# Moving GpSimd's arithmetic to VectorE, and building the low parts of the attention weights by accumulating DMA

## The chip, the core and the metric

The kernel runs on one core of a Trainium2 chip. The core has a matrix engine (TensorE, "PE" in the profile), VectorE ("DVE"), ScalarE ("ACT"), GpSimd ("POOL"), and SyncE ("SP"), which here only issues DMAs. Each engine works through its own queue in order and waits at semaphores for the others. The metric is the device time of one execution in microseconds; lower is better.

## What is computed

The reference is one inference step of a two-layer decoder, in float32, over 512 prompt tokens and 8 x 8 sample tokens:

```python
rq, rk, rv, rg, sq, sk, sv, mq, g_r, g_s, g_m = in_proj(xp, w_in[l], pos_p)
ret_o, s_p = retention_prompt(rq, rk, rv)            # per head pair
swa_o = swa_prompt(sq, sk, sv, attn_sinks[l])        # window 128
mk, mv = mem_kv(mem_prompt, w_mem_kv[l])
mem_o = mem_attend(mq, mk, mv)
ret_b = (silu(rg) * group_norm(ret_o, gn_g)) @ w_br_ret
swa_b, mem_b = swa_o @ w_br_swa, mem_o @ w_br_mem
merged = sigmoid(g_r) * ret_b + sigmoid(g_s) * swa_b + sigmoid(g_m) * mem_b
x = layer_norm(ALPHA * x + merged @ w_out, ln1_g, ln1_b)
h = square(relu(x @ w_up))
x = layer_norm(ALPHA * x + h @ w_down, ln2_g, ln2_b)
```

The model width is 1024. The sample tokens go through the same weights with caches of their own. The weights of a layer are some 80 MB, and nearly all the work is the product of the 576 tokens with them.

## The kernel before

**Units.** The weights of a layer are cut into 154 units of 128 x 1024 float32 (512 KB). `unit_order` gives their sequence: mk, mv (memory keys and values, four each); for each of four head pairs rk, rq, rv, rv, rg, rg; sv, sk, sq; gr and br; mq; gs, bs, gm, bm; wo (eight); then for four chunks of the MLP eight up and eight dn. "Unit u" counts through both layers. Tokens are handled as two groups, A and B, of 288 columns each.

**Precision.** PE multiplies in the format fp32r, which keeps fewer bits than float32. So each operand is split into a rounded high part and a low part, the rest. `gemm` does three matmuls for each of a unit's eight slots: high by high, low by high, high by low. The unit's low part is therefore needed from its second matmul on.

**The life of a unit.** `fetch` (L516) lets SP load the raw unit. `split` (L522) makes high and low. For up and dn units the high part is a copy on ACT, the low part is first -raw by an ACT activation with scale -1, and then a DMA issued by POOL adds the raw unit to it: an accumulating DMA. (The scaled copy is rounded as the high part is, so raw added to it leaves the rest.) For all other units `split_into` is used with `flexible=True`: `rounded` casts on ACT or DVE, and `pick` has the subtraction done on DVE or POOL.

**What sets the order.** The program is written by a builder that keeps a clock of its own: `Clock` gives every operation a cost and an end on its engine, `Filler` writes side work (attention, norms) between the matmuls when its inputs are due by that clock. `rounded` and `pick` choose the engine that would be done sooner by that clock. `tick` writes the next split when ACT is free by the clock, but a unit may be at most `cap` ahead of the last one whose matmuls are finished (3 in the attention part, up to 5 in the MLP). If PE's code comes to a unit that is not yet split, `run` writes the split there. Units are fetched two ahead of the split. Once written, the order is fixed, and the chip follows it in every queue.

**Side work that the change touches.** `norm_ev` (L701) is the LayerNorm spread over the last projection: accumulations, squares, the shift and the affine step. `retention` (L877) has four masked copies `vz` on POOL for each head pair. The rest are splits of activations in the memory attention, the MLP and elsewhere.

**Tiles.** All large tiles have the tag T, in a ring of 38 buffers. pg and pa are PSUM banks, u and t are small tiles, and accA, accB, rc, s and ln belong to the norm. Since every operation is written through the helper `Timed`, all rows carry its line, L337, and the tiles and shapes have to tell them apart.

Of the kernel before, what the change touches and what calls it, by code (L numbers as in the profile page):

```python
# [8 lines left out]
F32 = mybir.dt.float32  # L9
# [15 lines left out]
EPS = 1e-5  # L25
# [396 lines left out]
class Builder:  # L422
# [75 lines left out]

    def pick(self, *ins, bias=0.0):
        n = ins[0].free_size()  # L500
        return self.soonest((("vector", 0.068 + n / 960.0 + bias), ("gpsimd", 0.15 + n / 480.0)), *ins)

    def rounded(self, hi, src):
# [4 lines left out]
    def split_into(self, hi, lo, src, flexible=False):  # L508
        if flexible:
            self.rounded(hi, src)  # L510
        else:
            self.nc.scalar.copy(hi, src)
        e = self.pick(hi) if flexible else self.nc.vector
        e.tensor_tensor(lo, src, hi.bitcast(F32), ALU.subtract)

# [6 lines left out]
    def split(self, u):  # L522
        raw = self.raw.pop(u)
        k = unit_order()[u % UNITS]
        hi = self.tile([P, 8, P], F32R)
        lo = self.tile([P, 8, P], F32R)
        if k[0] in ("up", "dn"):
            self.nc.scalar.copy(hi, raw)
            self.nc.scalar.activation(lo, raw, AF.Copy, scale=-1.0)
            self.nc.gpsimd.dma_start(lo, raw, accum_op=ALU.add)  # L530
        else:
            self.split_into(hi, lo, raw, True)
        self.w[u] = (hi, lo)
# [166 lines left out]

    def norm_ev(self, g, y, l, gi, eps, out, scale=None, bias=1.0):  # L701

# [23 lines left out]
        def shift():  # L726
            pm = self.bank("a")[:, :n]
            yield from mean(pm, st["acc"])
            yield (pm,)
            st["c"] = self.u(n)  # L730
            V.tensor_scalar(st["c"], pm, 4.0, None, ALU.mult)
            cb = st["c"].unsqueeze(1).to_broadcast([P, 4, n])
            self.pick(y[1], st["c"], bias=bias).tensor_tensor(y[1], y[1], cb, ALU.subtract)

        def half():
            c = st.pop("c")
            V.tensor_tensor(y[0], y[0], c.unsqueeze(1).to_broadcast([P, 4, n]), ALU.subtract)
# [4 lines left out]
            self.pick(sq[:, 0:2], sq[:, 2:4], bias=bias).tensor_tensor(sq[:, 0:2], sq[:, 0:2], sq[:, 2:4], ALU.add)  # L742
            self.pick(sq[:, 0], sq[:, 1], bias=bias).tensor_tensor(sq[:, 0], sq[:, 0], sq[:, 1], ALU.add)
            self.pick(st["s2"], sq[:, 0], bias=bias).tensor_tensor(st["s2"], st["s2"], sq[:, 0], ALU.add)

        def last():
# [28 lines left out]
            def mult(i):  # L775
                j, k = pieces[i]
                if i == 2 and out is not None:
                    V.tensor_tensor(y[1], y[1], mb, ALU.subtract)
                e = G if i == 3 and out is None else V
                e.tensor_tensor(y[j][:, k], y[j][:, k], rb, ALU.mult)  # L780
                return y[j][:, k]
# [8 lines left out]
            def end(i):  # L790
                j, k = pieces[i]
                for q in (k.start, k.start + 1):
                    affine(4 * j + q, y[j][:, q], y[j][:, q], V)
                h = out[g]["h"][j][:, k]
                self.pick(y[j][:, k], h).tensor_tensor(out[g]["l"][j][:, k], y[j][:, k], h.bitcast(F32), ALU.subtract)
            if out is not None:
# [28 lines left out]
        def ev(m, ps):  # L825
# [7 lines left out]
            if m == 0:  # L833
# [4 lines left out]
                return  # L838
            self.pick(yt, st["acc"], bias=0.0 if m in (1, 7) else bias).tensor_tensor(st["acc"], st["acc"], yt, ALU.add)
            if m == 1:  # L840
                st["shift"] = shift()
                self.fill.add(st["shift"], 1)
            if m == 4:
                st["s2"] = self.tile([P, 512], tag={"A": "s", "B": "rc"}[g], bufs=1)[:, :n]
                S.activation(st["s2"], yt, AF.Square)
                st["half"] = half()
                self.fill.add(st["half"], 1)
            elif m > 4:
                sq = self.u(n)
                S.activation(sq, yt, AF.Square)  # L850
                if m == 7:
                    self.fill.finish(st["half"])
                if m == 7:
                    self.fill.flush()
                    self.pick(sq, st["s2"]).tensor_tensor(st["s2"], st["s2"], sq, ALU.add)
                    st["last"] = last()
                    self.fill.add(st["last"], 0)
                else:
                    self.fill.later(lambda: self.pick(sq, st["s2"], bias=bias).tensor_tensor(st["s2"], st["s2"], sq, ALU.add),
                                    2.0, sq)  # L860
# [16 lines left out]
    def retention(self, l, p, qk, rv, rvs, sg, GR):  # L877
# [159 lines left out]
        for g_ in "AB":  # L1037
            src = wt[:, :, OFF[g_]:OFF[g_] + NG[g_]]
            hi, lo = GR[g_]["h"][h0 // 4][:, m:m + 2, :], GR[g_]["l"][h0 // 4][:, m:m + 2, :]
            S.copy(hi, src)  # L1040
            yield (hi,)
            self.pick(src, hi, bias=1.0).tensor_tensor(lo, src, hi.bitcast(F32), ALU.subtract)

# [29 lines left out]
    def hi_lo(self, hi, lo, src):  # L1073

        self.nc.scalar.copy(hi, src)
        yield (hi,)
        e = self.nc.vector if src.space == PSUM else self.pick(src, hi)
        e.tensor_tensor(lo, src, hi.bitcast(F32), ALU.subtract)

# [134 lines left out]
    def mem_prompt(self, h, mq, mk, mv, ME):  # L1214
# [7 lines left out]
        for i, g in enumerate("AB"):  # L1222
            src, hi = mq[g][:, h, POFF[g]:POFF[g] + 256], q[:, 0, i * 256:(i + 1) * 256]
            self.rounded(hi, src)
            yield (hi,)
            self.pick(src, hi).tensor_tensor(q[:, 1, i * 256:(i + 1) * 256], src, hi.bitcast(F32), ALU.subtract)
        yield Pe((q, mk[1]))
# [115 lines left out]
    def layer(self, l, X):  # L1343
# [224 lines left out]
        def mem_parts():  # L1568
            for parts, src in ((mk, mkd), (mv, mvd)):
# [5 lines left out]
                yield (parts[0],)  # L1575
                self.pick(t, parts[0]).tensor_tensor(parts[1], t, parts[0].bitcast(F32), ALU.subtract)
        self.fill.add(mem_parts(), 2)
# [84 lines left out]
        for c in range(4):  # L1662
            H = self.feat_tiles(2)

            def up_ev(m, H=H):
                def ev(g, ps):
# [5 lines left out]
                    lo = H[g]["l"][m // 4][:, m % 4, :]  # L1672
                    self.fill.later(lambda: self.pick(r, h).tensor_tensor(lo, r, h.bitcast(F32), ALU.subtract),
                                    4.0 if m < 6 else 1.5, h)
# [25 lines left out]
            if c < 3:  # L1700
# [4 lines left out]
                continue  # L1705
            n2 = {g: self.norm_ev(g, y[g], l, 16, EPS, X2, bias=0.0 if g == "A" and X2 is None else 1.0) for g in "AB"}
            if X2 is not None:
# [89 lines left out]
```

## Time and profile before

| | |
|---|---|
| Time, median of three runs | 2206.06 us (2203.5 to 2207.72) |
| Profiled execution | 2201.67 us, its span 2199.6 us |
| Busy: PE, DVE, ACT, POOL | 98%, 49%, 39%, 18% of the span |
| Matmuls | 16,468 |
| DMA | 284.56 MB, mean 129 GB/s |
| Accumulating DMAs by POOL | 128 |

The profile is one execution, recorded by the hardware profiler. A row of a timeline gives the start, the duration, the engine, the operation with its output and inputs, and in brackets how long the engine was idle before and what released it. Neighbouring operations of one form stand in one row, with their count behind x; their duration is then from the first start to the last end. Where PE is nearly always busy, its list of waits shows the places where another engine is late.

### The profile page before, as it was taken

What the parts mean: (1) busy time and instruction counts of PE and PEld (TensorE: products, weight loads), DVE (VectorE), ACT (ScalarE), POOL (GpSimd) and SP (SyncE); (2) the same over time, 40 slices, a digit from 0 to 9 for tenths busy, and PEclk for the clock granted to TensorE, in tenths of its full rate; (3) what the DMA queues carried; (4) which work ended last, traced back from release to release, by engine and by line L of the source; (5) the groups of instructions that cost most, each with busy time, mean ns of one, the idle gap of its engine ahead of it and who ended that gap; (6) DMA issues with size and microseconds to landing.
All of it is one profiled execution on the core that took longest, in us unless ns stands there. A gap on an engine that the chain in (4) does not pass through costs nothing.

```text
span 2199.6 us, 39261 instructions
## 1 busy us (share of the span) xinstructions
PE 2153.1 (98%) x16468; PEld 2091.5 (95%) x16468; DVE 1071.2 (49%) x2186; ACT 847.7 (39%) x1581; POOL 388.2 (18%) x384
## 2 busy tenths in 40 slices
PE   9999999999999999999989999999999999999997
PEld 9999899999999999999989998999899999999996
DVE  6666866455567111111766668564455661111127
ACT  3222234222247454536432221342222474637362
POOL 0232300011023111111422223000110231111113
PEclk9999999999999999999999999999999999999998
DMA  8222211334355857686442222113342557686761
GB/s 301 82 84 98 82 50 67 116 108 141 107 169 124 202 146 181 159 202 158 126 164 82 99 74 92 49 58 116 134 152 90 164 131 188 157 195 153 176 149 48
DMA packets 85168, 284.56 MB, mean 129 GB/s; under 512 B 9280, under 2 KB 19008, under 8 KB 84928
## 3 DMA queue, kind: packets, MB, share of 16 engines
q1 hardware_dynamic: 50944, 168.27, 21.9%
q0 software_dynamic: 28960, 105.92, 21.6%
q10 hardware_dynamic: 5088, 7.87, 1.1%
q8 instruction: 129, 2.11, 0.4%
q14 instruction: 47, 0.39, 0.1%
HBM read 200.89 MB, written 15.99 MB: 99 GB/s over the span
## 4 chain that ended last, share of the span: by engine, by line
PE 87%; DVE 8%; DMA 2%; issue 1%; ACT 1%; POOL 1%; SPq 0%; DVEq 0%; POOLq 0%; ACTq 0%
PE pg L337 78%; PE pa L337 9%; DVE T L337 4%; DVE u L337 2%; ACT T L337 1%; DMA T<-in_mcv 0%; DVE ln L337 0%; DMA T<-in_wall 0%; DMA T<-in_mck 0%; POOL T L337 0%; DMA T<-T 0%; DMA T<-in_swk 0%; DMA T<-in_memT 0%; ACT u L337 0%; DVE accA L337 0%
## 5 line engine op out<-in xcount | busy, mean ns | idle before, releaser
L337 PE MATMUL pg<-T,T 128*128 128x288 f32 (+1 forms) x14432 | 1958.3, 296 | 18.2 <-DVE T L337 15.9
L337 PEld LDWEIGHTS pg<-T,T 128*128 128x128 f32 x14432 | 1925.0, 188 | 41.4 <-DVE T L337 18.2
L337 ACT CAST T<-T 128x1024 fp32r<-128x1024 f32 (+5 forms) x358 | 307.7, 883 | 267.3 <-issue 83.7
L337 DVE TENSOR_TENSOR T<-T,T 128x1024 fp32r<-128x1024 f32 (+5 forms) x248 | 271.7, 1104 | 83.1 <-ACT T L337 71.9
L337 DVE TENSOR_TENSOR T<-u,T 128x288 fp32r<-128x288 f32 x150 | 68.6, 457 | 317.7 <-ACT T L337 311.5
L337 POOL DMA_DIRECT2D T<-T x128 | 110.6, 864 | 616.6 <-ACT T L337 517.1
L337 ACT ACTIVATE t<-pg 128x288 f32<-128x288 f32 x128 | 52.7, 412 | 295.8 <-PE pg L337 295.4
L337 POOL TENSOR_TENSOR T<-T,T 128x1024 fp32r<-128x1024 f32 (+2 forms) x43 | 91.3, 2135 | 413.0 <-ACT T L337 350.8
L337 ACT ACTIVATE T<-T 128x1024 fp32r<-128x1024 f32 (+1 forms) x140 | 148.7, 1064 | 24.4 <-DMA T<-T 11.8
L337 DVE TENSOR_TENSOR T<-T,pg 128x288 f32<-128x288 f32 x112 | 50.5, 453 | 202.9 <-PE pg L337 202.4
L337 PE MATMUL pa<-T,T 128*32 128x128 f32 (+8 forms) x1064 | 121.7, 319 | 9.5 <-DMA T<-in_mck 4.2
L337 PEld LDWEIGHTS pa<-T,T 128*32 128x32 f32 (+3 forms) x1064 | 83.5, 148 | 32.4 <-issue 15.0
L337 ACT ACTIVATE u<-pg 128x288 f32<-128x288 f32 x128 | 52.5, 410 | 153.0 <-PE pg L337 153.0
L337 DVE TENSOR_TENSOR T<-T,u 128x288 f32<-128x288 f32 (+2 forms) x132 | 92.8, 713 | 4.0 <-POOL accB L337 0.3
L337 ACT CAST T<-u 128x288 fp32r<-128x288 f32 x160 | 69.6, 435 | 49.3 <-DVE u L337 45.2
L337 DVE SCALAR_TENSOR_TENSOR T<-T,pg 128x288 f32<-128x288 f32 x48 | 21.7, 453 | 91.2 <-PE pg L337 91.2
L337 ACT COPY T<-pg 128x512 f32<-128x512 f32 (+2 forms) x44 | 21.0, 479 | 111.6 <-PE pg L337 111.6
L337 ACT ACTIVATE u<-u 128x288 f32<-128x288 f32 x128 | 57.1, 446 | 4.0
L337 POOL TENSOR_TENSOR T<-T,cst 128x512 fp32r<-128x512 f32 x32 | 43.7, 1394 | 79.8 <-ACT T L337 59.8
L337 ACT ACTIVATE T<-pa,rnb,rr 128x128 f32<-128x128 f32 x32 | 12.1, 459 | 116.4 <-DVE rnb L337 81.9
L337 DVE SCALAR_TENSOR_TENSOR u<-t,pg 128x288 f32<-128x288 f32 x64 | 28.9, 452 | 55.7 <-PE pg L337 55.5
L337 DVE SCALAR_TENSOR_TENSOR T<-t,pg 128x288 f32<-128x288 f32 x64 | 28.9, 451 | 51.4 <-ACT t L337 42.9
(159 smaller groups left out, 1101.5 us busy)
## 6 DMA issues: line engine op xcount, KB each, us to landing
T<-in_wall SPq DMA_DIRECT2D x305, 512.0 KB, 3.5
T<-T POOLq DMA_DIRECT2D x128, 512.0 KB, 5.4
T<-in_mck POOLq DMA_DIRECT2D x16, 512.0 KB, 3.8
T<-in_mcv POOLq DMA_DIRECT2D x16, 512.0 KB, 6.8
T<-in_s POOLq DMA_DIRECT2D x8, 512.0 KB, 4.1
out_state_s<-T POOLq DMA_DIRECT2D x8, 512.0 KB, 3.1
T<-in_xT SPq DMA_DIRECT2D x4, 576.0 KB, 10.9
T<-in_xT ACTq DMA_DIRECT2D x4, 576.0 KB, 6.5
```

What stands on the lines that cost most here:

```text
L337: r = f(*a, **kw)
```

## The change

All arithmetic on POOL goes to DVE: `pick` is gone, and each of its uses, the four `vz` copies of each head pair and the two explicit POOL steps of the norm are now DVE operations. Every unit after the eight mk and mv units of layer 0 is split in the way of the up and dn units: copy and scaling on ACT, accumulating DMA by POOL. That is 172 units more. Caps, fetches, tiles and matmuls are the same.

```diff
-    def pick(self, *ins, bias=0.0):
-        n = ins[0].free_size()
-        return self.soonest((("vector", 0.068 + n / 960.0 + bias), ("gpsimd", 0.15 + n / 480.0)), *ins)
...
-        e = self.pick(hi) if flexible else self.nc.vector
-        e.tensor_tensor(lo, src, hi.bitcast(F32), ALU.subtract)
+        self.nc.vector.tensor_tensor(lo, src, hi.bitcast(F32), ALU.subtract)
...
-        if k[0] in ("up", "dn"):
+        if u > 7:
             self.nc.scalar.copy(hi, raw)
             self.nc.scalar.activation(lo, raw, AF.Copy, scale=-1.0)
             self.nc.gpsimd.dma_start(lo, raw, accum_op=ALU.add)
...
-            self.pick(y[1], st["c"], bias=bias).tensor_tensor(y[1], y[1], cb, ALU.subtract)
+            self.nc.vector.tensor_tensor(y[1], y[1], cb, ALU.subtract)
...
-                G.tensor_tensor(y[1], y[1], mb, ALU.subtract)
+                V.tensor_tensor(y[1], y[1], mb, ALU.subtract)
...
-                nc.gpsimd.tensor_tensor(
+                V.tensor_tensor(
                     vz[i][:, e], v2[:, i, e * P:(e + 1) * P].bitcast(F32).unsqueeze(1).to_broadcast([P, 4, P]),
```

Some ten more lines replace `self.pick(...)` by `self.nc.vector` in the same way.

In the whole program DVE has 138 subtractions of 128x1024 and 63 casts fewer and takes some 115 operations from POOL; ACT has 172 scalings and 61 casts more; POOL has 158 arithmetic operations fewer and 172 DMAs more. As costs and engines in the builder's clock change, operations are also written in another order. Three places:

ACT, second head pair of layer 0, from the evacuation of its rv units (the COPY to u) on. Casts of 128x1024 are the high parts of units, `t<-pg` the evacuations of rg units. Before, the second rg unit (rg3) was split on DVE here, and the first CAST is that of rk2:

```order
L337 COPY u_1241<-pg_1224 64x256
L337 CAST T_1265<-T_1088 128x1024
L337 ACTIVATE t_1281<-pg_1244 128x288
L337 ACTIVATE t_1309<-pg_1284 128x288
L337 CAST T_1321<-T_1251 128x1024
L337 ACTIVATE t_1343<-pg_1312 128x288
L337 ACTIVATE t_1371<-pg_1346 128x288
```

and now:

```order
L337 COPY u_1252<-pg_1235 64x256
L337 CAST T_1264<-T_955 128x1024
L337 ACTIVATE T_1265<-T_955 128x1024
L337 CAST T_1283<-T_1098 128x1024
L337 ACTIVATE T_1284<-T_1098 128x1024
L337 ACTIVATE t_1294<-pg_1255 128x288
L337 ACTIVATE t_1322<-pg_1297 128x288
```

The split of rg3 (first CAST and ACTIVATE) and that of rk2 both stand on ACT behind that COPY, ahead of the evacuations of rg2.

ACT at the start, around the evacuation of mv (COPY to T from pg) and the transposed mk (COPY from pa). Before:

```order
L337 CAST T_331<-T_265 128x1024
L337 COPY T_154<-pg_289 128x512
L337 COPY T_154<-pg_290 128x512
L337 COPY T_401<-pa_396 128x512
L337 COPY T_409<-pa_404 128x512
L337 CAST T_420<-T_327 128x1024
L337 CAST T_432<-T_347 128x1024
```

and now:

```order
L337 CAST T_331<-T_265 128x1024
L337 CAST T_351<-T_303 128x1024
L337 ACTIVATE T_352<-T_303 128x1024
L337 COPY T_154<-pg_289 128x512
L337 COPY T_154<-pg_290 128x512
L337 COPY T_402<-pa_397 128x512
L337 COPY T_410<-pa_405 128x512
L337 CAST T_421<-T_327 128x1024
L337 ACTIVATE T_422<-T_327 128x1024
```

The cast and scaling of rk0 stand ahead of the four COPYs, which DVE did before; those of rq0 (the last two rows) stand behind them, as its cast did.

ACT at the layer boundary, beginning at the evacuations of mk0 and mk1 of layer 1 (COPY T<-pg 128x256: mk0 to mk3; `ln`: the norm of group B). Before, from the row behind the COPY of mk0, with the CASTs of mk3, mv0, mv1, mv2 and mv3:

```order
L337 CAST T_11693<-T_11455 128x1024
L337 COPY T_11642<-pg_11674 128x256
L337 CAST T_11719<-T_11488 128x1024
L337 COPY T_11642<-pg_11710 128x256
L337 CAST t_11751<-rc_11525 128x288
L337 COPY T_11642<-pg_11742 128x256
L337 ACTIVATE ln_11776<-pa_11653 128x288
L337 ACTIVATE ln_11789<-u_11786 128x288
L337 ACTIVATE ln_11789<-ln_11789 128x288
L337 CAST T_11795<-T_11691 128x1024
L337 CAST T_11826<-T_11717 128x1024
L337 CAST T_11838<-T_11793 128x1024
```

and now:

```order
L337 COPY T_11719<-pg_11723 128x256
L337 COPY T_11719<-pg_11749 128x256
L337 CAST T_11784<-T_11557 128x1024
L337 ACTIVATE T_11785<-T_11557 128x1024
L337 COPY T_11719<-pg_11775 128x256
L337 CAST t_11818<-accB_11193 128x288
L337 CAST t_11831<-rc_11606 128x288
L337 ACTIVATE ln_11837<-pa_11816 128x288
L337 ACTIVATE ln_11842<-u_11839 128x288
L337 ACTIVATE ln_11842<-ln_11842 128x288
L337 CAST T_11848<-T_11579 128x1024
L337 ACTIVATE T_11849<-T_11579 128x1024
```

The split of mk3 comes after the COPY of mk1 rather than before it; mv0 is cast after the three `ln` steps rather than after mk1, and the splits of mv1 to mv3 follow behind the eight affine steps. At wo2 and wo3 the order of before stays, with a scaling behind each CAST.

## Rows read from the trace of the kernel before

**Rows 1.** Busy us, share, instructions: the page's part 1.

```profile
PE 2153.1 (98%) x16468; PEld 2091.5 (95%) x16468; DVE 1071.2 (49%) x2186; ACT 847.7 (39%) x1581; POOL 388.2 (18%) x384
```

**Rows 2.** What PE waited for, whole span: us, times, longest.

```profile
PE pg L337 <- DVE T L337: 15.9, 10, 4.2
PE pa L337 <- DMA T<-in_mck: 4.2, 4, 1.8
PE pa L337 <- DMA T<-in_mcv: 3.2, 2, 1.8
```

**Rows 3.** Timeline 256:284: start, us, engine, operation, count [idle before <-releaser].

```profile
256.90 0.45 DVE L337 TENSOR_TENSOR u<-u,rope 128x288 f32<-128x288 f32 x1
...
257.10 10.63 PE L337 MATMUL pg<-T,T 128*128 128x288 f32 x78
...
259.47 10.81 POOL L337 TENSOR_TENSOR T<-T,T 128x1024 fp32r<-128x1024 f32 x5
...
260.61 10.00 DVE L337 TENSOR_TENSOR u<-u,rope 128x288 f32<-128x288 f32 x1
...
271.90 11.92 PE L337 MATMUL pg<-T,T 128*128 128x288 f32 x78 [4.17 <-DVE T L337]
```

**Rows 4.** Groups by form: busy us, mean ns | idle before.

```profile
L337 DVE TENSOR_TENSOR T<-T,T 128x1024 fp32r<-128x1024 f32 x152 | 208.9, 1380 | 34.4 <-ACT T L337 25.4 <-PE pa L337 5.7 <-DVE T L337 0.5
```

**Rows 5.** Timeline 683:702, one split of the MLP on its new path.

```profile
684.65 1.05 ACT L337 ACTIVATE T<-T 128x1024 fp32r<-128x1024 f32 x1
...
686.00 0.87 POOL L337 DMA_DIRECT2D T<-T  x1 [0.34 <-ACT u L337]
```

**Rows 6.** DMA issues 685:687: KB each, us to landing.

```profile
T<-T POOLq DMA_DIRECT2D x1, 512.0 KB, 4.8
```

**Rows 7.** DMA issues, whole span: count, KB each, median us to landing.

```profile
T<-T POOLq DMA_DIRECT2D x128, 512.0 KB, 5.4
...
T<-in_s POOLq DMA_DIRECT2D x8, 512.0 KB, 4.1
```

**Rows 8.** Timeline 106:116, around the second rg unit of a pair.

```profile
108.96 1.05 ACT L337 CAST T<-T 128x1024 fp32r<-128x1024 f32 x1
...
115.08 0.41 ACT L337 ACTIVATE t<-pg 128x288 f32<-128x288 f32 x1 [2.79 <-PE pg L337]
```

**Rows 9.** Timeline 24:30, the cast of rk0 of layer 0.

```profile
25.48 0.69 DVE L337 CAST T<-T 128x1024 fp32r<-128x1024 f32 x1
```

**Rows 10.** Timeline 30:70, first matmuls of rk0.

```profile
29.79 0.83 PE L337 MATMUL pg<-T,T 128*128 128x288 f32 x5
```

**Rows 11.** DMA issues 0:50: count, KB each, median us to landing.

```profile
d<-T POOLq DMA_DIRECT2D x2, 512.0 KB, 11.1
```

**Rows 12.** What PE waited for, 1083:1130.

```profile
PE pg L337 <- DVE T L337: 6.9, 6, 2.7
```

**Rows 13.** Timeline 1090:1124, the layer boundary.

```profile
1097.23 0.37 ACT L337 COPY T<-pg 128x256 f32<-128x256 f32 x1
...
1102.44 0.86 PE L337 MATMUL pg<-T,T 128*128 128x256 f32 x5 [2.68 <-DVE T L337]
...
1106.03 0.42 ACT L337 ACTIVATE ln<-pa 128x288 f32<-128x288 f32 x1
...
1107.80 2.93 ACT L337 CAST T<-T 128x1024 fp32r<-128x1024 f32 x3
...
1116.56 2.19 ACT L337 ACTIVATE T<-T,par 128x288 fp32r<-128x288 f32 x4 [5.82 <-DVE T L337]
```

**Rows 14.** Timeline 626:636, the first wo units.

```profile
627.21 2.00 ACT L337 CAST T<-T 128x1024 fp32r<-128x1024 f32 x2
...
630.58 0.45 DVE L337 SCALAR_TENSOR_TENSOR T<-T,pg 128x288 f32<-128x288 f32 x1
```

More of the change, by code (lines that the diff above doesn't have):

```diff
@@ L699, in rsqrt, with norm_ev @@
             V.scalar_tensor_tensor(out, a, 1.5, out, ALU.add, ALU.mult)
-    def norm_ev(self, g, y, l, gi, eps, out, scale=None, bias=1.0):
+    def norm_ev(self, g, y, l, gi, eps, out, scale=None):
         nc = self.nc
@@ L741, in half @@
             V.scalar_tensor_tensor(st["acc"], c, -4.0, st["acc"], ALU.mult, ALU.add)
-            self.pick(sq[:, 0:2], sq[:, 2:4], bias=bias).tensor_tensor(sq[:, 0:2], sq[:, 0:2], sq[:, 2:4], ALU.add)
-            self.pick(sq[:, 0], sq[:, 1], bias=bias).tensor_tensor(sq[:, 0], sq[:, 0], sq[:, 1], ALU.add)
-            self.pick(st["s2"], sq[:, 0], bias=bias).tensor_tensor(st["s2"], st["s2"], sq[:, 0], ALU.add)
+            self.nc.vector.tensor_tensor(sq[:, 0:2], sq[:, 0:2], sq[:, 2:4], ALU.add)
+            self.nc.vector.tensor_tensor(sq[:, 0], sq[:, 0], sq[:, 1], ALU.add)
+            self.nc.vector.tensor_tensor(st["s2"], st["s2"], sq[:, 0], ALU.add)
         def last():
@@ L778, in mult @@
                     V.tensor_tensor(y[1], y[1], mb, ALU.subtract)
-                e = G if i == 3 and out is None else V
-                e.tensor_tensor(y[j][:, k], y[j][:, k], rb, ALU.mult)
+                V.tensor_tensor(y[j][:, k], y[j][:, k], rb, ALU.mult)
                 return y[j][:, k]
@@ L794, in end @@
                 h = out[g]["h"][j][:, k]
-                self.pick(y[j][:, k], h).tensor_tensor(out[g]["l"][j][:, k], y[j][:, k], h.bitcast(F32), ALU.subtract)
+                self.nc.vector.tensor_tensor(out[g]["l"][j][:, k], y[j][:, k], h.bitcast(F32), ALU.subtract)
             if out is not None:
@@ L838, in ev @@
                 return
-            self.pick(yt, st["acc"], bias=0.0 if m in (1, 7) else bias).tensor_tensor(st["acc"], st["acc"], yt, ALU.add)
+            self.nc.vector.tensor_tensor(st["acc"], st["acc"], yt, ALU.add)
             if m == 1:
@@ L854, in ev @@
                     self.fill.flush()
-                    self.pick(sq, st["s2"]).tensor_tensor(st["s2"], st["s2"], sq, ALU.add)
+                    self.nc.vector.tensor_tensor(st["s2"], st["s2"], sq, ALU.add)
                     st["last"] = last()
@@ L858, in ev @@
                 else:
-                    self.fill.later(lambda: self.pick(sq, st["s2"], bias=bias).tensor_tensor(st["s2"], st["s2"], sq, ALU.add),
+                    self.fill.later(lambda: self.nc.vector.tensor_tensor(st["s2"], st["s2"], sq, ALU.add),
                                     2.0, sq)
@@ L1041, in retention @@
             yield (hi,)
-            self.pick(src, hi, bias=1.0).tensor_tensor(lo, src, hi.bitcast(F32), ALU.subtract)
+            self.nc.vector.tensor_tensor(lo, src, hi.bitcast(F32), ALU.subtract)
     def softmax_swa(self, sb, ng, sink):
@@ L1076, in hi_lo @@
         yield (hi,)
-        e = self.nc.vector if src.space == PSUM else self.pick(src, hi)
-        e.tensor_tensor(lo, src, hi.bitcast(F32), ALU.subtract)
+        self.nc.vector.tensor_tensor(lo, src, hi.bitcast(F32), ALU.subtract)
     def swa_prompt(self, l, c, sq, sk, sv, SW):
@@ L1225, in mem_prompt @@
             yield (hi,)
-            self.pick(src, hi).tensor_tensor(q[:, 1, i * 256:(i + 1) * 256], src, hi.bitcast(F32), ALU.subtract)
+            self.nc.vector.tensor_tensor(q[:, 1, i * 256:(i + 1) * 256], src, hi.bitcast(F32), ALU.subtract)
         yield Pe((q, mk[1]))
@@ L1575, in mem_parts @@
                 yield (parts[0],)
-                self.pick(t, parts[0]).tensor_tensor(parts[1], t, parts[0].bitcast(F32), ALU.subtract)
+                self.nc.vector.tensor_tensor(parts[1], t, parts[0].bitcast(F32), ALU.subtract)
         self.fill.add(mem_parts(), 2)
@@ L1672, in ev @@
                     lo = H[g]["l"][m // 4][:, m % 4, :]
-                    self.fill.later(lambda: self.pick(r, h).tensor_tensor(lo, r, h.bitcast(F32), ALU.subtract),
+                    self.fill.later(lambda: self.nc.vector.tensor_tensor(lo, r, h.bitcast(F32), ALU.subtract),
                                     4.0 if m < 6 else 1.5, h)
@@ L1705, in layer @@
                 continue
-            n2 = {g: self.norm_ev(g, y[g], l, 16, EPS, X2, bias=0.0 if g == "A" and X2 is None else 1.0) for g in "AB"}
+            n2 = {g: self.norm_ev(g, y[g], l, 16, EPS, X2) for g in "AB"}
             if X2 is not None:
```

## The prediction, made before the changed kernel ran

> **What bounds the kernel now.** The busy times come first: PE is busy for 98% of the span, DVE for 1071 us and ACT for 848 us of 2200 [rows 1]. Matmuls follow each other at 10.63 us for 78, 0.136 us each [rows 3], so a time can change only where PE waits or where matmuls take longer. The list of what PE waited for is therefore the second view: ten waits for DVE in the matmuls of the projections, 15.9 us in all and 4.2 at most, and six for two kinds of load of the memory caches, 4.2 and 3.2 us [rows 2]. The third is the timeline around the longest wait. POOL runs five TENSOR_TENSORs in 10.81 us, a DVE operation on 128x288 beside them takes 10.00 us, and PE waits 4.17 us for what follows it. The 78 matmuls after the wait take 11.92 us instead of 10.63, 1.3 us more [rows 3]. The other layer runs the same program, so I count this stretch twice.
>
> So this kernel leaves little to win, while any new wait of PE is paid in full. The question is whether the new split is ready in time at every unit.
>
> **What the new split takes.** Before, a unit's low part needed a cast (1.05 us on ACT [rows 8]) and a subtraction on DVE (mean 1.38 [rows 4]), some 2.4 us. Now it needs the cast, a scaling of 1.05 on ACT, 0.3 us until POOL issues the DMA, and the DMA to land: the scaling starts at 684.65, the DMA at 686.00 [rows 5]. Issue to landing took 4.8 us for this one [rows 6], and 5.4 is the median of the 128 of the MLP [rows 7]. From the cast's start, C = 0.95 + 1.35 + 4.8 = 7.1 us, 7.7 with the median. I take 7.1, since in the attention part few such DMAs run at once. In the MLP this is hidden by splits that run several units ahead. In the attention part a unit may be split at most three ahead of the last one finished, so the cover has to be looked for place by place.
>
> **What goes.** POOL's arithmetic goes and with it the 10 us operation: twice 4.2 of waiting and 1.3 of slower matmuls, **-11 us**, if POOL is what slowed DVE (a rival below). The six waits for memory loads, 7.4 us [rows 2], lie in a part whose order shifts both ways: the loads of the first set come earlier against their use, those of the second come in one burst. I book 0, with -7 and +7 as ends.
>
> **What comes, by place.**
> (1) The second rg unit of each head pair, 8 places. Its split is let go only when the pair's rv units are finished, and on ACT it stands behind the COPY that evacuates them (first pair of fences in the section on the change). In the trace ACT is free for a cast at 108.96, and PE begins this unit where the evacuation of rg2 starts, 115.08 [rows 8]: 6.0 us of cover against C = 7.1. Before, the shorter DVE path fitted in. The wait is 1.1 with C = 7.1 and 1.7 with 7.7; I take 1.3, so 8 x 1.3 = **+10** (7 to 14).
> (2) The start. The raw rk0 is there at 25.48, where DVE casts it, and PE begins it at 29.79 [rows 9, 10]. With the new path the DMA is issued at 25.5 + 2.3 = 27.8. In this stretch the DMA engines are loaded: stores that POOL issues land in 11.1 us [rows 11]. Landing between 4.8 and 11.1 gives a wait of 3 to 9; I take 8 us of landing, 6 of wait. Then rq0: ACT casts it only behind two COPYs of transposes that PE does after the first matmuls of rk0 (the second pair of fences), about 2.7 us after PE goes on, while PE needs rq0 after one unit and the transposes, 48 x 0.136 + 0.8 = 7.3 us. The cover is 4.6 against 2.3 + 8: 5.5 us at most, and 2.5 with a landing of 4.8. I take 5. Together **+11** (5 to 16).
> (3) The layer boundary, where the first units of layer 1 are split beside the LayerNorm. PE waited 6.9 us for DVE there before, in six waits [rows 12]. In the new order (the third pair of fences) the cast of mk3 stands behind the COPY of mk1, which ends at 1097.6 [rows 13]: ready at 1097.6 + 7.1 = 1104.7, while PE stood at mk3 at 1099.8 (it went on at 1102.44 after 2.68 [rows 13]), a wait of 5. The cast of mv0 now stands behind the norm's three "ln" operations, which began 3.6 us after mk3 went on and lasted 1.8 [rows 13]: 1104.7 + 5.4 + 7.1 = 1117.2, while PE comes to mv0 at about 1104.7 + 3.9 = 1108.6, a wait of 8 to 9. The cast of mv1 stands behind eight affine operations, 2.19 us for four [rows 13]; they end about 1118 or later, so mv1 is ready near 1125 and PE is there near 1120: 5 to 6. For mv2 and mv3, issued one behind the other on POOL, 1.5 together. With the middle of each, 5 + 8.5 + 5.5 + 1.5 = 20.5, less the 6.9 of before: **+14** (7 to 22).
> (4) Unit wo2 in both layers. ACT casts wo2 and wo3 from 627.21, and the evacuation at 630.58 is where PE turns to wo2 [rows 14]. On the new path wo2 is ready at 627.2 + 7.1 = 634.3: a wait of 3.7, and 4.3 with the median landing. wo3 then has as much again as cover. 2 x 4 = **+8** (7 to 11).
>
> At the other units the split stands at least one unit (48 x 0.136 = 6.5 us) further ahead than in (1) and (4); I book nothing there. Where that cover is gone, a unit costs C less what is left of it.
>
> **What does not decide.** ACT gains 172 scalings of 1.05 and 61 casts: 848 + 181 + 64 = 1093 us, half of the span. DVE loses 138 subtractions of 1.38 (190 us) and gets about 115 operations of POOL, none dearer than these: 880 to 1040 us. Neither engine becomes the bound as a whole. POOL's queue now has 172 DMA issues of 0.87 us [rows 5] in place of 158 operations.
>
> **The sum.** -11 + 10 + 11 + 14 + 8 = +32. The profiled execution took 2201.67 us, so its like would take 2234. It stood 4.4 below the median of 2206.06; on the median I predict **2238 us**.
>
> **The rivals.**
> *Not slower: the new waits are shorter than the old ones.* With a landing like that of a plain load that POOL issues in retention, 4.1 us [rows 7], C is 6.4, and by the same covers the waits are 8 x 0.4 + 2 x 3 + (2.1 + 1.8) + 12, some 25. It takes a C near 5.5 to bring them to 15, and if then also all waits for DVE and memory loads go (15.9 + 7.4 + 2.6 of slower matmuls, 26 [rows 2, 3]), the kernel gains about 11: 2195 us. It decides where the new waits sum to less than what goes, 11 to 26. For it: much of DVE's lateness is POOL's doing. Against it: no accumulating DMA in the rows lands under 4.8, and PE's places in (1) and (4) are fixed. I give 0.14 to faster, and 0.07 to a balance within 0.2%, which is 4.4 us and about what a measurement of this kernel can tell from no change.
> *Dearer: the DMAs land late.* If the landing is 8 us as in the loaded start, also elsewhere, C is 10.3: (1) costs 8 x 4.3, (4) 2 x 6.9, (2) stays at 11 and (3) grows by 3.2 at some three units, to 24. That is 83, less 11: 2278 us. For it: POOL issues in order, and the raw loads share the DMA engines with twice as many transfers. Against it: the loads that POOL issues in retention beside a busy DVE land in 4.1 [rows 7], and the casts of the splits leave DVE with this change. I give it 0.13. The Trainium skill, page "SBUF — State Buffer", section "Who interferes with whom", has a rule that speaks for this rival: a DMA that looks stalled by a DVE operation is one that GpSimd issues, and it waits because GpSimd cannot write its descriptors while DVE holds their shared port. By an example of the page, in which 620 ns become 3100, each of the new DMAs would land 2.5 us later, an estimate of 37 us more at the 15 units named above, +69 in all. The 4.1 us of the rows show nothing of it.
> *DVE is slow there without POOL.* Then the -11 does not come: 2249 us, and the change does half of what it says. Against it speaks that the same form takes 0.45 us in its use before it [rows 3]. 0.06.
>
> **How the numbers follow.** My forecast has 0.60, the rivals 0.14, 0.07, 0.13 and 0.06. The ends of the terms give -18 + 7 + 5 + 7 + 7 = +8 and -4 + 14 + 16 + 22 + 11 = +59, so 2214 to 2265 for the forecast itself. To leave out no more than 2 in 10 the range reaches into both sides: 2205 to 2275. Slower has 0.60 + 0.13 + 0.06 = 0.79.
>
> **What will show it.** In the list of what PE waited for, a row with the releaser DMA T<-T should lead, some 30 waits and 35 to 50 us, and the row for DVE should fall to a few us. At the unit after each pair's rv a wait of 1 to 2 us should stand eight times; at wo2 one of about 4; at the start and the layer boundary several of 4 to 9. The 10 us DVE operation should be gone. I am wrong if the waits for DMA T<-T sum to less than 15, if the long waits stand at units that I gave cover, or if DVE or ACT becomes what PE waits for.

## The result and the profile after

The changed kernel takes 2272.89 us (median of four runs, 2272.54 to 2273.47) against 2206.89 in the same comparison: a ratio of 1.0302, 95% interval 1.0284 to 1.0319. It is 66 us slower. The forecast was 2238 us, 32 us slower, in a range of 2205 to 2275. The direction was right, and the time lies in the range near its upper end, but the loss is a little more than twice the one forecast. The profiled execution took 2273.47 us, its span 2271.2, 71.6 more than the span before. (The profiled execution of the kernel before, 2201.67 us, was 5.2 us below the median, so the account by place adds up to 71.6 us and not to 66.)

The page after, part 1 (busy us, share, instructions), answers [rows 1]:

```profile
PE 2179.7 (96%) x16468; PEld 2108.6 (93%) x16468; DVE 850.9 (37%) x2115; ACT 1062.1 (47%) x1810; POOL 311.7 (14%) x398
```

PE is busy 26.6 us longer with the same 16,468 matmuls, and idle 45.0 us longer (91.5 against 46.5). So more than a third of the loss is matmuls that take longer. DVE and ACT end at 851 and 1062 us, against 880 to 1040 and 1093 in the prediction; neither is a bound. DVE ends below its range: the estimate left out the casts that leave it, and the 52 operations `u<-u,rope` take 23.3 us instead of 42.4 without POOL's arithmetic beside them. By the rows of both traces DVE gives up 141 subtractions of 128x1024 and 57 casts and takes over 127 operations, where the section on the change has 138, 63 and some 115.

What PE waited for in the kernel after (us, times, longest) answers [rows 2]:

```profile
PE pg L337 <- DMA T<-T: 52.4, 19, 7.1
PE pa L337 <- DVE T L337: 9.0, 8, 2.7
PE pa L337 <- DMA T<-in_mcv: 5.5, 7, 1.5
PE pa L337 <- DMA T<-in_mck: 2.9, 3, 1.4
PE pa L337 <- ACT u L337: 2.8, 2, 1.4
PE pg L337 <- DVE T L337: 1.8, 6, 0.4
```

The list turned over as predicted: the waits of the projections for DVE fell from 15.9 to 1.8 us, and 19 waits for the accumulating DMAs, 52.4 us, lead. They are fewer and longer than the 30 waits of the prediction. In the small attention matmuls (pa) the waits for DVE grew from 2.0 to 9.0 us, and 2.8 for ACT's tile u are new. The cache loads stand at 8.4, where 7.4 stood before, but at another place: before, PE waited for the first set of them (480 to 499 us in layer 0), now nearly all of it is for the second (573 to 583).

DMA issues after (count, KB each, median us to landing) answer [rows 7]:

```profile
T<-in_wall SPq DMA_DIRECT2D x305, 512.0 KB, 4.9
T<-T POOLq DMA_DIRECT2D x300, 512.0 KB, 5.4
T<-in_mck POOLq DMA_DIRECT2D x16, 512.0 KB, 6.9
...
T<-in_s POOLq DMA_DIRECT2D x8, 512.0 KB, 8.0
```

and before:

```profile
T<-in_wall SPq DMA_DIRECT2D x305, 512.0 KB, 3.5
...
T<-in_mck POOLq DMA_DIRECT2D x16, 512.0 KB, 3.8
```

The accumulating DMAs land in 5.4 us in the median as before. What became later is the traffic beside them: POOL's own loads, in_mck from 3.8 to 6.9 and in_s from 4.1 to 8.0, and the weight loads from 3.5 to 4.9. Within the 300 of this trace the landing goes with what is in flight when POOL issues the DMA: with no other transfer the median is 4.6 us (89 DMAs), with one 5.4 (109), with two 6.1 (53), with three 8.4 (28), with four or more 10.2 (21).

Now the places. For each named unit I subtract the start of its first matmul in the trace before from that in the trace after; the growth of this difference over a stretch is what the stretch lost:

| Stretch | forecast | measured, layer 0 and layer 1 | of it PE idle |
|---|---|---|---|
| (2) start, rk0 to rv0 | +11 | +16.3 | +11.8 |
| (1) the four head pairs of each layer | +10 | +4.5, +3.7 | +3.4, +2.7 |
| sq units (POOL beside DVE) | -11 | -5.7, -5.9 | -4.2, -4.1 |
| memory attention, first gr unit to gm2 | 0 (-7 to +7) | +10.6, +11.9 | +4.5, +6.3 |
| gm2 to wo0 (bm3) | 0 | +6.2, +5.5 | +3.5, +3.7 |
| (4) wo2 | +8 | +4.0, +4.0 | +2.7, +2.8 |
| (3) layer boundary, to rg0 of layer 1 | +14 | +17.9 | +14.1 |
| the rest | 0 | -1.4 | -2.2 |
| sum | +32 | +71.6 | +45.0 |

What is not idle time is matmuls that take longer. At the four places (1) to (4) PE's idle time grew by 37.6 us, less than the 43 forecast; the longer matmuls add 12.8.

The first unit, rk0, in the timeline after, with the answering rows of before in [rows 9, 10]:

```profile
28.16 1.00 POOL L337 DMA_DIRECT2D T<-T  x1 [27.72 <-ACT T L337]
...
37.37 1.57 PE L337 MATMUL pg<-T,T 128*128 128x288 f32 x5 [7.09 <-DMA T<-T]
...
51.82 4.46 PE L337 MATMUL pg<-T,T 128*128 128x288 f32 x18 [4.71 <-DMA T<-T]
```

The DMA issued at 28.16 is waited for until 37.37: landing 9.2 us in the loaded start, against the 8 that I took. PE waited 7.09 here and 4.71 for rq0. What the granted clock did behind the two waits stands in the windows of the trace (stretch, length, busy us of PE, PEld, DVE, ACT, POOL, then the granted clock, DMA share, GB/s):

```profile
37.40:41.00 3.60, 3.60 (x16) 3.58 (x17) 0.00 (x0) 0.91 (x2) 0.29 (x1) 0.50 1.02 419
...
51.80:55.00 3.20, 3.18 (x13) 3.19 (x14) 0.00 (x0) 0.00 (x0) 0.00 (x0) 0.50 1.07 211
```

In these 3.6 and 3.2 us the clock is granted at 0.50, that is 1.2 instead of 2.4 GHz; in the windows behind them (41.00:44.50 and 55.00:60.00) the mean is 0.83 and 0.91. Before these stretches PE had been idle for 7.09 and 4.71 us.

The second rg unit of a pair, against [rows 8]:

```profile
126.56 1.05 ACT L337 CAST T<-T 128x1024 fp32r<-128x1024 f32 x1
...
127.51 1.06 ACT L337 ACTIVATE T<-T 128x1024 fp32r<-128x1024 f32 x1
...
128.87 0.87 POOL L337 DMA_DIRECT2D T<-T  x1 [23.76 <-ACT T L337]
...
133.47 0.80 PE L337 MATMUL pg<-T,T 128*128 128x288 f32 x4 [0.69 <-DMA T<-T]
```

Cast at 126.56, DMA at 128.87, ready at 133.47: C = 6.9 us, with 4.6 from issue to landing. PE waited 0.69. At the eight places the waits were 0.65 to 1.36 us, and the next unit began 0.9 to 1.6 us later for it.

The layer boundary, against [rows 12, 13]:

```profile
1141.41 1.44 PE L337 MATMUL pg<-T,T 128*128 128x256 f32 x5 [6.21 <-DMA T<-T]
...
1152.11 4.33 PE L337 MATMUL pg<-T,T 128*128 128x512 f32 x12 [5.29 <-DMA T<-T]
...
1163.09 2.50 PE L337 MATMUL pg<-T,T 128*128 128x512 f32 x5 [6.65 <-DMA T<-T]
```

mk3 waits 6.21, mv0 5.29, mv1 6.65: the three that were predicted, with 5, 8.5 and 5.5. Two more, of 1.47 and 1.50 us, stand at the first two rv units of layer 1, whose DMAs landed after 10.7 and 10.8 us. And mv1 was held on POOL:

```profile
1153.57 1.05 ACT L337 ACTIVATE T<-T 128x1024 fp32r<-128x1024 f32 x1
...
1156.62 0.75 POOL L337 DMA_DIRECT2D d<-T  x1 [2.23 <-DVE T L337]
1157.37 2.73 POOL L337 DMA_DIRECT2D T<-T  x3
```

Its scaling ended at 1154.62, but its DMA, the first of the three, left at 1157.37, behind a store (d) that waited for DVE.

The chain of side work of the second set of sampled tokens' memory attention, which no part of the prediction had priced:

```profile
563.24 1.06 ACT L337 ACTIVATE T<-T 128x1024 fp32r<-128x1024 f32 x1
...
564.60 0.87 POOL L337 DMA_DIRECT2D T<-T  x1 [8.97 <-ACT T L337]
565.15 1.43 POOL L337 DMA_DIRECT2D T<-in_mck  x2
...
566.23 1.40 POOL L337 DMA_DIRECT2D T<-in_mcv  x2
...
573.75 0.64 PE L337 MATMUL pa<-T,T 128*32 128x256 f32 x8 [1.32 <-DMA T<-in_mck]
...
581.12 1.08 PE L337 MATMUL pa<-T,T 128*32 128x128 f32 x16 [1.48 <-DMA T<-in_mcv]
```

POOL stands idle for 8.97 us in front of an accumulating DMA whose scaling on ACT ends at 564.3. Only behind it, at 565.15, does it issue the loads of the keys (in_mck) and then those of the values, and PE waits for both. No wait here is longer than 1.5 us, but there are many, and the matmuls between them run slowly. The windows of the stretch from the first gr unit to gm2 in layer 0, before and after, and of 574 to 586 after:

```profile
282.86:566.69 283.83, 278.75 (x2245) 264.77 (x2244) 157.00 (x322) 91.92 (x234) 17.33 (x22) 0.99 0.31 105
...
298.26:592.66 294.40, 284.79 (x2245) 268.01 (x2243) 112.76 (x281) 134.17 (x279) 39.23 (x52) 0.97 0.61 160
...
574.00:586.00 12.00, 7.29 (x81) 4.15 (x74) 3.06 (x13) 1.71 (x5) 0.00 (x0) 0.53 0.77 298
```

PE is busy 6.0 us longer with the same matmuls, and idle 4.5 us longer. From 574 to 586 PE is busy for 7.29 of 12 us, at a mean clock of 0.53.

And bm3, the last unit before wo:

```profile
637.04 0.86 POOL L337 DMA_DIRECT2D T<-T  x1 [8.66 <-ACT t L337]
...
647.61 15.54 PE L337 MATMUL pg<-T,T 128*128 128x288 f32 x96 [3.45 <-DMA T<-T]
```

Issued at 637.04, waited for until 647.61. The DMA issues of 634 to 650 say what ran beside it:

```profile
T<-in_wall SPq DMA_DIRECT2D x5, 512.0 KB, 12.4
T<-T POOLq DMA_DIRECT2D x3, 512.0 KB, 10.5
T<-in_xT ACTq DMA_DIRECT2D x1, 576.0 KB, 16.3
```

All kinds of transfer are late there, with the loads of x for the residual, four of 576 KB that ACT issues from 632.25 on (the last of them lies in this window).

### The profile page after: what moved, and what is told of

Read it like the earlier page. It is cut to its first block, busy times and chain, and to the rows that moved or that the text cites. A ratio compares the mean times of both kernels' runs of the same rounds, so it can differ in the third digit from the quotient of the medians.

```text
span 2271.2 us, 39690 instructions
## 1 busy us (share of the span) xinstructions
PE 2179.7 (96%) x16468; PEld 2108.6 (93%) x16468; DVE 850.9 (37%) x2115; ACT 1062.1 (47%) x1810; POOL 311.7 (14%) x398
## 3 DMA queue, kind: packets, MB, share of 16 engines
q0 software_dynamic: 53728, 196.11, 42.4%
## 4 chain that ended last, share of the span: by engine, by line
PE 70%; issue 18%; DMA 7%; DVE 2%; ACT 1%; POOL 1%; SPq 0%; ACTq 0%; POOLq 0%; DVEq 0%
PE pg L337 63%; PE pa L337 7%; DMA T<-T 4%; DVE T L337 2%; DMA T<-in_wall 2%; DMA T<-in_mcv 1%; ACT T L337 1%; POOL T L337 1%; DVE u L337 0%; SPq L337 0%; ACTq L337 0%; DMA T<-in_swk 0%; DVE ln L337 0%; ACT ln L337 0%; DVE accB L337 0%
## 5 line engine op out<-in xcount | busy, mean ns | idle before, releaser
L337 PE MATMUL pg<-T,T 128*128 128x288 f32 (+1 forms) x14432 | 1977.8, 297 | 55.0 <-DMA T<-T 52.4
L337 POOL DMA_DIRECT2D T<-T x300 | 259.1, 867 | 1755.7 <-ACT T L337 1460.5
L337 ACT CAST T<-T 128x1024 fp32r<-128x1024 f32 (+5 forms) x419 | 368.7, 894 | 253.5 <-issue 123.8
L337 ACT ACTIVATE T<-T 128x1024 fp32r<-128x1024 f32 (+1 forms) x312 | 330.4, 1060 | 33.9 <-DMA T<-T 16.1
L337 PE MATMUL pa<-T,T 128*32 128x128 f32 (+8 forms) x1064 | 128.8, 338 | 16.7 <-DVE T L337 7.9
L337 ACT ACTIVATE u<-pg 128x288 f32<-128x288 f32 x128 | 52.4, 409 | 152.7 <-PE pg L337 152.7
L337 DVE TENSOR_TENSOR T<-T,T 128x576 fp32r<-128x576 f32 (+5 forms) x119 | 77.9, 675 | 44.9 <-ACT T L337 42.8
L337 DVE TENSOR_TENSOR T<-T,u 128x288 f32<-128x288 f32 (+2 forms) x136 | 88.1, 660 | 3.6
L337 DVE TENSOR_TENSOR T<-pa,T 128x512 fp32r<-128x512 f32 (+2 forms) x48 | 25.4, 535 | 67.1 <-ACT T L337 58.8
L337 ACT CAST T<-pa 128x256 fp32r<-128x256 f32 (+2 forms) x36 | 15.1, 418 | 73.0 <-PE pa L337 69.0
```

Source lines behind the costliest of these rows:

```text
L337: r = f(*a, **kw)
```

## The experiments

In the diffs, lines with - are those of the kernel that an experiment starts from.

**The two parts apart.** First POOL's arithmetic alone:

```diff
-        if u > 7:
+        if k[0] in ("up", "dn"):
```

> One part alone: POOL's arithmetic goes to DVE, but only the up and dn units keep the accumulating DMA; the attention units are cast on ACT or DVE and subtracted on DVE. Theory (the whole loss is in the new split, the move itself gains): the waits at the sq units go, about 12 us less than before, 2195 us, and no wait for DMA T<-T over 1 us. Rival (DVE, which takes over POOL's share, is late itself): 2207 us or more, with the row of waits for DVE at or above its 15.9 us.

Measured: 2229.25 us, ratio 1.0101 (1.0084 to 1.0118). The sq units gained 5.7 and 5.9 us, as in the whole change, and yet the kernel lost. What PE waited for in this kernel:

```profile
PE pg L337 <- DVE T L337: 17.1, 9, 5.5
PE pg L337 <- DMA T<-T: 13.6, 4, 5.2
PE pa L337 <- DMA T<-in_mcv: 9.0, 4, 4.0
PE pa L337 <- DMA T<-in_mck: 8.8, 4, 4.0
```

There are four waits for accumulating DMAs at the sixth and seventh up unit of each layer, up to 5.2 us long, and later waits at the layer boundary. This met the rival's number. Whether DVE is the cause or the order that the builder writes with the new costs was open. Then the other part alone, from the kernel before:

```diff
-        if k[0] in ("up", "dn"):
+        if u > 7:
```

> The other part alone: the attention units are split by the accumulating DMA, and the arithmetic that POOL had besides (norm, vz, activations) stays with it. Theory: the loss comes whole from the split, 2273 us, or up to 12 us more because POOL's queue now holds arithmetic ahead of the DMAs. Rival (the loss needs both parts, because DVE is late with the operations that it took over): 2255 us or less.

Measured: 2269.49 us, ratio 1.0281 (1.0265 to 1.0296). The loss of the whole change is there without the move. The parts do not add up (21 + 62 against 66); as each of these kernels has an order of its own, that too pointed at the order.

**One place undone.** In the changed kernel:

```diff
-        if u > 7:
+        if u > 11:
```

> The changed kernel, with the first four units of the attention part of layer 0 (rk, rq, rv, rv of the first pair) split in the old way, subtracted on DVE. In the changed kernel PE waited 7.3 and 4.9 us at the first two, and rv came 16.7 us later than before. Theory (a long wait costs its length, and the slower matmuls behind it 4.6 us more): 2256 us. Rival 1 (only the waits count): 2261 us. Rival 2 (the time is lost again at the next place, since loads and DMAs then crowd there): 2268 us or more.

Measured: 2256.96 us, 15.9 less than the changed kernel, against 16.7 in the theory and 11.8 of waiting proper. The slower matmuls behind the waits are part of the price.

**All named places undone**, 28 of the 172 units (so 144 accumulating DMAs remain, two more than the text on record says):

```diff
-        if u > 7:
+        late = u < UNITS + 12 and (u < 12 or u >= UNITS) or k[0] == "rg" and k[1] % 2 or k in (("bm", 3), ("wo", 2))
+        if not late:
```

> The changed kernel, with the old split (subtraction on DVE) for the named units alone: the first four of layer 0, the first twelve of layer 1, the second rg unit of each pair, wo2 and bm3. Theory (cover, place by place): these places cost 16.7 + 8.1 + 17.9 + 8 + 11.7 = 62 us, so 2211 us, with the memory part of the sampled tokens still some 22 us slower than before. Rival (the number of accumulating DMAs and the load on the DMA engines cost, not the place): 142 of the 172 remain, so above 2255 us.

Measured: 2218.7 us, ratio 1.005 (1.0035 to 1.0065). Of 66 us, 54 hang on these 28 units. What is left is 11 us of loss, with the 11 of gain at the sq units in it: the memory part still loses 10 and 13 us, as in the changed kernel. At the layer boundary 4.9 of the 17.9 us remain, with PE's longest wait for DVE (5.5 us, at mv2): that much of the boundary is not the DMA's.

**Order or path?** The order of PE's work comes from the builder's clock, so it can be held fixed while the operations change. This kernel charges the clock as the kernel before did and lets DVE do what POOL did:

```diff
-        return self.soonest((("vector", 0.068 + n / 960.0 + bias), ("gpsimd", 0.15 + n / 480.0)), *ins)
+        e = self.soonest((("vector", 0.068 + n / 960.0 + bias), ("gpsimd", 0.15 + n / 480.0)), *ins)
+        return self.dve_as(e.name)
+
+    def dve_as(self, name):
+        return Timed(self.nc.vector.eng, name, self.clock)
...
-                nc.gpsimd.tensor_tensor(
+                self.dve_as("gpsimd").tensor_tensor(
```

> The order in which PE's work is written is kept as in the kernel before (the builder's clock is charged as before), and only POOL's arithmetic runs on DVE; the attention units keep the subtraction, now always on DVE. The move alone had cost 21 us with the order that the builder then wrote. Theory (that loss came from the new order, and DVE itself has the time): the waits at the sq units go and nothing comes, 2195 us. Rival (DVE is late with the operations that it took over, whatever the order): 2207 us or more, with waits for DVE at the layer boundary or the first up units.

Measured: 2190.16 us, ratio 0.993 (0.9915 to 0.9945). It is faster than before, by a little more than the theory. By the rows of the traces PE's matmuls stand in the order of the kernel before, but for 10 of 16,468. What PE waited for:

```profile
PE pg L337 <- DVE T L337: 7.8, 8, 3.7
PE pa L337 <- DVE T L337: 6.9, 12, 0.7
PE pa L337 <- DMA T<-in_mck: 4.8, 4, 2.2
```

So DVE has the time. The 39 us between this kernel and the first one lie in the order that the builder wrote there, with the choice of ACT or DVE for some 20 casts that goes with it. If the order does that much, it might also explain the memory part of the change. Hence the whole change in the old order, built on the kernel just shown:

```diff
-            self.split_into(hi, lo, raw, True)
+            n = raw.free_size()
+            e = self.soonest((("scalar", 0.094 + n / 1200.0), ("vector", 0.2 + n / 1920.0)), raw)
+            if u > 7:
+                self.nc.scalar.eng.copy(hi, raw)
+                self.nc.scalar.eng.activation(lo, raw, AF.Copy, scale=-1.0)
+                self.nc.gpsimd.eng.dma_start(lo, raw, accum_op=ALU.add)
+                self.clock.op(e.name, "copy", hi, [raw], {}, False)
+                self.clock.op(self.pick(hi).name, "tensor_tensor", lo, [raw, hi], {}, False)
+            else:
+                self.split_into(hi, lo, raw, True)
```

> The whole change (POOL's arithmetic on DVE, accumulating DMAs for all units after the first eight), with the written order of PE's work of the kernel before. Theory (the part of the sampled tokens' memory attention, +22 us in the changed kernel, is due to the new order, in which a chain of side work is forced out in one piece; the places with too little cover stay): 2251 us. Rival (the chain is slow because ACT and POOL are held by the new splits, in any order): 2268 us or more.

Measured: 2295.94 us, ratio 1.0407 (1.0392 to 1.0423), 23 us worse than the changed kernel. The theory fell. The order that the builder writes for the new splits is the better one for them.

```profile
PE pg L337 <- DMA T<-T: 53.6, 19, 11.3
PE pa L337 <- DMA T<-in_mcv: 18.9, 8, 4.2
PE pa L337 <- DMA T<-in_mck: 8.6, 4, 3.7
PE pa L337 <- DMA T<-in_swk: 7.3, 2, 4.7
```

The cache loads that POOL issues are waited for 27.5 us here, against 8.4 in the changed kernel, and in_swk for another 7.3. The reverse, in the order of the changed kernel:

```diff
-            self.nc.scalar.activation(lo, raw, AF.Copy, scale=-1.0)
-            self.nc.gpsimd.dma_start(lo, raw, accum_op=ALU.add)
+            if k[0] in ("up", "dn"):
+                self.nc.scalar.activation(lo, raw, AF.Copy, scale=-1.0)
+                self.nc.gpsimd.dma_start(lo, raw, accum_op=ALU.add)
+            else:
+                self.nc.vector.eng.tensor_tensor(lo, raw, hi.bitcast(F32), ALU.subtract)
+                self.clock.op("scalar", "activation", lo, [raw], {"scale": -1.0}, False)
+                self.clock.op("gpsimd", "dma_start", lo, [raw], {}, False)
```

> The reverse: the written order of PE's work of the changed kernel, but the low parts of the attention units are subtracted on DVE right behind the cast, without scaling or DMA. Theory (covers are lost to the DMA's path, the memory part to the order): no wait for DMA T<-T outside the MLP, and some 20 us lost in the memory part, 2217 us. Rival 1 (the memory part's loss needs the new splits too): 2200 us or less. Rival 2 (the order costs more than the path): 2240 us or more.

Measured: 2194.01 us, ratio 0.9947 (0.9933 to 0.9962). Rival 1: the changed kernel's order costs about 4 us against the old one, and its whole loss, 79 us from here, needs the scaling and the DMA. PE's matmuls stand in the order of the changed kernel throughout. These two apart, in the same order:

```diff
-                self.nc.vector.eng.tensor_tensor(lo, raw, hi.bitcast(F32), ALU.subtract)
-                self.clock.op("scalar", "activation", lo, [raw], {"scale": -1.0}, False)
+                self.nc.scalar.activation(lo, raw, AF.Copy, scale=-1.0)
+                self.nc.vector.eng.tensor_tensor(lo, raw, hi.bitcast(F32), ALU.subtract)
```

> The written order of the changed kernel, cast and scaling on ACT as there, but the low part is then subtracted on DVE (the scaled values are overwritten), and no DMA is issued for the attention units. Without the scaling this took 2194 us. Theory (the loss comes from the DMA's landing and from POOL's queue, little from ACT's second pass): up to 10 us more, 2194 to 2204 us. Rival (ACT's second pass delays the side work and the splits behind it): 2225 us or more.

Measured: 2209.09 us, ratio 1.0013 (1.0004 to 1.0023). It lies between the two. The scaling brings 15 of the 79 us, more than the theory's 10, and the DMAs in place of the subtractions the other 64. More than half of the 15 is this experiment's own, though: by the traces 8.7 us of it lie at wo2, where DVE's subtraction waits for the scaling that it overwrites, the norm's sum (accA) stands on DVE behind that subtraction, and PE waits 3.39 us for what follows it, against 1.31 in the kernel without the scaling. In the changed kernel no subtraction stands there. So ACT's second pass alone is worth less than 15 us.

**POOL's queue.** In the changed kernel, with the order of PE's work unchanged:

```diff
-        self.nc.gpsimd.dma_start(t, self.I[name][l, b])
+        Timed(self.nc.sync.eng, "gpsimd", self.clock).dma_start(t, self.I[name][l, b])
```

> The changed kernel in its own order, with the loads of the memory caches issued by SP instead of POOL, where they stand behind accumulating DMAs that wait for ACT. Theory (the chain of side work is late by its order): within 5 us of the changed kernel, 2268 to 2278 us. Rival (POOL's queue holds the cache loads up): the waits for in_mck and in_mcv go, 2260 us or less.

Measured: 2257.88 us, 15.0 less (the profiled execution, 2252.51, was the fastest of four). The rival was right. The timeline of this kernel at the same place:

```profile
556.63 1.92 SPq L337 DMA_DIRECT2D T<-in_mck  x2
...
569.10 1.93 PE L337 MATMUL pa<-T,T 128*32 128x256 f32 x32
...
574.03 1.74 PE L337 MATMUL pa<-T,T 128*32 128x128 f32 x56 [0.36 <-DVE T L337]
```

The loads of the keys leave at 556.63 rather than 565.15, and the runs of matmuls on keys and values are no longer interrupted by loads. The memory part loses 0.7 and 2.3 us instead of 10.6 and 11.9, with the operations of PE, ACT and DVE in the same order. Both findings together, on the changed kernel (the two edits above):

> The changed kernel with the old split at the named units (2219 us) and with the cache loads on SP (which gave 15 us in the changed kernel). Theory (both causes stand beside each other and add up): 2203 us, no longer slower than before. Rival (the cache loads only waited because of the late units, the same loss counted twice): 2213 us or more.

Measured: 2201.23 us, ratio 0.9979 (0.9969 to 0.9988). They add up (54 and 15 alone, 72 together): with 144 accumulating DMAs still in the attention part, the kernel is no slower than before.

**bm3.** In the changed kernel the loads of x move one step ahead:

```diff
-            if i == 3:
+            if i == 2:
                 steps.append(([], load_y, 0.0))
```

> The changed kernel, with the four loads of x for the residual (576 KB each, ACT's queue) one step earlier, so that they no longer run beside the accumulating DMA of bm3, which landed after some 10.5 us there. Theory (shared DMA engines make it late): the wait at bm3, 3.5 us in both layers and the slower matmuls behind it, goes, 2262 us. Rival (bm3 has too little cover anyway): 2270 us or more.

Measured: 2270.55 us, 2.3 less than the changed kernel; by the time, the rival. The trace shows more. The DMAs of bm2 and bm3 in this kernel, issues of 616 to 618 and of 637 to 639, and that of bm2 in the changed kernel, issues of 615 to 617:

```profile
T<-T POOLq DMA_DIRECT2D x1, 512.0 KB, 8.9
```

```profile
T<-T POOLq DMA_DIRECT2D x1, 512.0 KB, 5.7
```

```profile
T<-T POOLq DMA_DIRECT2D x1, 512.0 KB, 4.8
```

In the changed kernel it was 4.8 for bm2 and 10.5 for bm3. The late landing moved with the loads from bm3 to bm2, and the wait with it (2.00 at bm2, none at bm3). So the loads beside it do make it late, and they hit whichever unit stands there. The time hardly fell because the wait moved: 3.8 and 1.5 us are now lost at bm2, and at wo2 6.1 and 5.8 instead of 4.0 and 4.0, since PE came to it 3.8 us earlier in layer 0 and its DMA landed only 1.7 us earlier.

**The fastest version.** The kernel in the old order with DVE (2190.16), and in addition the cache loads on SP:

> The fastest version so far (written order of before, POOL's arithmetic on DVE, attention units subtracted on DVE), with the loads of the memory caches issued by SP. Theory (POOL's queue held them up there too): the six waits for in_mck and in_mcv, 7 us, go, 2183 us. Rival (SP's weight loads queue behind them, or the loads are short of time in any queue): 2188 us or more.

Measured: 2188.31 us, ratio 0.9918 (0.9902 to 0.9935), not to be told from 2190.16. The waits for in_mck say more than the time, which stands at the rival's threshold: 3.9 of 4.8 us remain, so without accumulating DMAs in the attention part POOL's queue was not what held these loads. Both versions beat the kernels before and after.

## Why the prediction was right or wrong

*The reading of what bounds the kernel* was right: little to win, and every new wait paid in full, and then some by the slower matmuls behind it.

*The gain of 11 us at the sq units* came, 11.6, and with it the reason: the operation of 10 us [rows 3] takes 0.45 when POOL has no arithmetic. The third rival (DVE slow without POOL) is out.

*The new path, C = 7.1 us*, was 6.9 in the head pairs. Places (1) and (4), priced with it, came at 8.2 and 8.0 against 10 and 8.

*The start and the layer boundary* were mis-sized, 16.3 against 11 and 17.9 against 14, but hardly in their waits: PE's idle time grew by 11.8 and 14.1 there. I left out that the clock is low behind a long wait; that is the other 4.5 and 3.8. (For rq0 the cover of 4.6 against 2.3 + 8 makes 5.7, not the 5.5 that stands there; the sum took 5.) The sum counted the slower matmuls for the gain at the sq units, but for none of the new waits, and over the program PE's busy time grew by 26.6 us. Undoing the start gave back 15.9 us for 11.8 of waiting. That the waits of the boundary fit is in part luck: mv0 waited 3.2 less than booked, mv1 stood in POOL's queue, and the 3.0 at the rv units were not in the sum.

*The step that failed* is the memory part, "I book 0, with -7 and +7 as ends": it cost 22.5 us. The -7 came: the six waits of before are all but gone. I looked at where the loads stand against their use in PE's order. I should have looked at what stands ahead of them in POOL's: an accumulating DMA that waits for ACT holds all loads behind it. The text passed over it with the remark that POOL's queue has 172 issues in place of 158 operations. The many short waits that came of it cost about as much again in slow matmuls. With the loads on SP 15 us came back.

*The second step that failed* is "I book nothing there", said of the other units because their split stands at least one unit further ahead. bm3 had a cover of some 9 us (its DMA left at 637.04, 2.3 behind the cast, and PE stood at it 3.45 before 647.61), enough for C = 6.9 but not for a landing of 10.5 beside the residual's loads: 11.7 us in both layers. It is a long wait at a unit that I gave cover, one of the signs that I named for being wrong. The rival "dearer" took late landings for all units alike. They came where other transfers were in flight, at the start, at bm3 and at the boundary (up to 14.3 us behind 1158), and singly elsewhere, where the cover took them.

*The chances*: slower had 0.79. That the time lies in the range is luck: its upper end was drawn for dearer waits at the named places and for late landings, and what carried the time there are two stretches that the sum had at nothing.

*The rule cited from the Trainium skill*, page "SBUF — State Buffer", section "Who interferes with whom", has a DMA issued by GpSimd starved of port time for its descriptors beside a DVE operation. The trace shows no such effect: with no other transfer in flight, the 57 accumulating DMAs that POOL issued while DVE was idle landed after 4.6 us in the median, and the 19 that it issued with DVE busy for more than half of the issue after 4.8.

What stays open: why the builder's order for POOL's arithmetic on DVE alone (2229) is so much worse than the old one (2190). The traces show where, at the sixth and seventh up unit, at the boundary and in the memory part, but not which of the moved operations does it. It also stays open how the 64 us or more of the DMAs divide between landing time and POOL's queue at each unit, and what part of the boundary's waits for DVE is the order's; the sums over places are shown, the single shares are not.

## What to carry to other kernels

A step moved to a longer path through more engines costs nothing where the work runs far ahead, and where something holds it back, what the path exceeds the lead by. So list the units by cover, not by count: here 28 of 172 units carried four fifths of the loss. A DMA that waits for another engine blocks every load behind it on its queue, so loads with a due time belong on a queue without such waits. And count the slower matmuls behind every long wait of PE and among many short ones, not the wait alone.

## What the hardware showed that was not expected

- Behind the first two waits at the start, of 7.09 and 4.71 us, the granted clock was 0.50 in windows of 3.6 and 3.2 us. In the memory part, from 574 to 586 us, where no wait was over 1.5 us but PE was busy for only 7.29 of 12, its mean was 0.53. Over the whole program PE was busy 26.6 us longer with the same matmuls.
- An accumulating DMA of 512 KB landed in 4.6 us in the median with no other transfer in flight at its issue, and in 10.2 with four or more. A burst of loads moved by one step moved the late landing with it.
- A VectorE operation of 0.45 us took 10 beside GpSimd's subtractions, and 0.45 again once these were gone.
